# The context states of the four heads: taken ahead of the linear attention or inside its loop

## The chip, the cores and the metric

The kernel runs on one core of one Trainium2 chip. The core has a matrix engine (TensorE, PE in the rows), a vector engine (DVE), an activation engine (ACT), a general engine (GpSimd, POOL) and SyncE (SP), which here issues nearly all transfers. Each engine works through its own list of instructions in a fixed order and waits by semaphores for the others. The metric is the device time of one execution in microseconds (us).

## The reference, cut to what matters

Two transformer blocks run one after the other on 1024 tokens of width 1024, all in fp32. The change lies in the second block. Its mixer projects the 1024 tokens and, with the same weights, 256 context tokens. Four heads of linear attention (128 keys, 128 values each, forward and backward) start from a state that is worked out from the context tokens alone:

```python
def hg_forget(z, lb):
    k = (1.0 - lb) * jax.nn.sigmoid(-z)
    logf = jnp.log(jnp.maximum(lb + (1.0 - lb) * jax.nn.sigmoid(z), TINY))
    return k, logf

def gla_final_state(k, v, logf):                      # the context's state, one per head and direction
    suffix = jnp.minimum(lax.cumsum(logf, axis=1, reverse=True) - logf, 0.0)
    return jnp.einsum('bthk,bthv->bhkv', k * jnp.exp(suffix), v)

def gla_chunk_scan(q, k, v, logf, s0):                # linear attention that starts from that state
...
    def step(s, inp):
        qc, kc, vc, gc = inp
        b = jnp.cumsum(gc, axis=2)
        inter = jnp.einsum('bhtk,bhkv->bhtv', qc * jnp.exp(b), s)
        diff = b[:, :, :, None, :] - b[:, :, None, :, :]
        decay = jnp.where(causal, jnp.exp(jnp.minimum(diff, 0.0)), 0.0)
        scores = jnp.einsum('bhtk,bhtsk,bhsk->bhts', qc, decay, kc)
        intra = jnp.einsum('bhts,bhsv->bhtv', scores, vc)
...
    _, o = lax.scan(step, s0.astype(F32), (to_chunks(q), to_chunks(k), to_chunks(v), to_chunks(logf)))

def second_block(x, c, ctx, c_ctx, ada_w, ada_b, w_in, hg_lb, ...):
...
        px = modulate(x, mx[0], mx[1]) @ w_in[l]              # 1024 tokens
        pc = modulate(ctx, mc[0], mc[1]) @ w_in_ctx           # 256 context tokens
...
        s_f = gla_final_state(kf_c, v_c, lff_c)
        s_b = gla_final_state(flip(kb_c), flip(v_c), flip(lfb_c))
        mix_x = token_mixers(px, hg_x, s_f, s_b, *mix_args)   # linear attention | short conv | spatial gate
        x_new = layer_norm(ALPHA * x + mx[2] * (mix_x @ w_out[l]), ln1_g[l], ln1_b[l])
...
```

The state of a head needs the context's two gates (`z_f`, `z_b`), their logarithms summed from the far end, and the context's values `v_c`; nothing in it depends on the 1024 tokens.

## The kernel before

Every large product is made of three fp32r matmuls, from the high and the low part of each operand. A weight piece (`piece`, 128 x 1024, 512 KB) is loaded into one of two raw buffers `wr`, cast by ACT into its high part `wh`, and subtracted by POOL and DVE in turn into its low part `wl`; there are four buffers of `wh` and four of `wl`. `gemm_Z` takes one piece through all 1024 tokens: 48 matmuls of 128x512 into a two-bank tile `ps_Z`, of which there are two. `gemm_T` with `ctxT` takes a piece through the 256 context tokens: 24 matmuls of 128x256.

The second block's mixer is in three parts:

- `block2_in` norms and transposes the context (`ctxT`), makes the values of all heads for tokens and context (four pieces `w2_i`, ten output tiles `ps_z`; the tokens' values go to DRAM as `v_dr`, the context's stay as `vc`), then runs `spatial_gate` (four pieces `w2_sg`, eight tiles `ps_z`).
- `hgrn` is the loop over the four heads. Each head makes two gates from `w2_h[h, 0]` and `w2_h[h, 1]`, in `log_gate` (L1435 to L1441: copy out of PSUM on ACT, Tanh and Ln on ACT with steps of DVE between, a maximum on POOL). From them come `LB` and `LE` (log gates), `b` and `e` (sums of 128 tokens, by scans on DVE), `ks` (sum of two exponentials). Then it works out the context state: the gates `cps`, from the same two weight pieces while they are in SBUF, a second `log_gate` on 512 columns, two scans, an Exp, four transposes, and four matmuls into `st`, which ACT copies into the first slot of `S[0]` and the last of `S[1]`. The query and the output gate come from `w2_h[h, 2]` and `w2_h[h, 3]`; eight state updates follow. `gla_scores` makes, for each half `n` of the tokens, eight score products into `ps_lv`: one plain, and seven levels, each of four subtractions on DVE (`kk` from `LB`, `LE`; `qq` from `b`, `e`), two Exp on ACT, a multiplication by q on POOL (L1590), four fp32 matmuls (eight passes in the trace, L1593), and a masked copy on DVE. `gla_out` makes the output of a half (24 matmuls, a norm, four transposes). After head 2, and between scores and outputs of head 3, `short_conv` runs three products of `gemm_Z`.
- `block2_out` is the output GEMM with the weights `w_out2`, the residual rows `xs0` to `xs7` and a norm. The first five `xs` tiles are loaded at head 3, into the room where `ctxT` and `vc` were; the others follow in `block2_out`.

The tiles `LB`, `LE`, `b`, `e`, `ks`, `lf`, `q`, `og`, `vh`, `S` have one buffer each, `kk`, `qq`, `pt`, `kt` two. The order on each engine isn't that of the text: a scheduler lays the instructions out ahead of time by its own estimates, as far as data and buffers allow, so that products of the next head stand among the scores of this one. On the chip that order is fixed.

## Time and profile before

| what | us |
|---|---|
| median of 3 runs (2631.08 to 2636.38) | 2634.54 |
| the profiled execution | 2632.81 |
| its span in the trace | 2630.4 |
| values and spatial gate, 1232 to 1347 | 115 |
| first products and gates of head 0, 1347 to 1410 | 63 |
| the heads from the first score product, 1410 to 1815 | 405 |
| output GEMM's start, 1815 to 1862 | 47 |

The stretches are cut by hand in the trace, at the first score product of each head (1410, 1507, 1611, 1726) and where the outputs of head 3 go over to the output GEMM. The rows themselves stand in a section of their own below. In a windows view each engine's busy time in the stretch is read against the stretch's length: the engine near the length bounds it, and where none is near, the stretch goes by waits between engines.

### The profile page before, as it was taken

The numbers are of one execution on the slowest core, as the hardware profiler recorded it, in microseconds if no ns is written. First come the engines' busy times: TensorE is split into PE (matmuls) and PEld (weight loads), VectorE is DVE, ScalarE is ACT, GpSimd is POOL, SyncE is SP. The second block draws the span as 40 slices with busy tenths as digits, with TensorE's granted clock in tenths as the row PEclk, the third lists the DMA queues.
The fourth block names the chain that finished last, engine by engine and source line by source line (L and its number), as shares of the span: only waits on it lengthen the run. The fifth ranks groups of instructions, "written<-read, shape, count | busy, mean of one in ns | idle before, by whom it ended". The sixth has DMA issues, their size and how long they took to land.

```text
span 2630.4 us, 31222 instructions
## 1 busy us (share of the span) xinstructions
PE 2454.8 (93%) x11558; PEld 1996.0 (76%) x11558; DVE 1816.2 (69%) x2634; ACT 1002.2 (38%) x1473; POOL 1260.8 (48%) x769
## 2 busy tenths in 40 slices
PE   7989998989999989999998889998988999999998
PEld 3867776867788778788787677876766888887886
DVE  7387656588888896655157766678868777778645
ACT  3324462533333333224325545453234333333221
POOL 3253142368888862122125535445255777773222
PEclk8998798999999989999999989998999999999999
DMA  6522116213444348554120101113311222226442
GB/s 242 150 64 56 26 52 236 99 39 132 139 137 140 129 159 295 199 200 154 66 69 27 40 13 53 53 61 125 139 57 56 88 80 89 73 102 263 163 144 88
DMA packets 119015, 295.71 MB, mean 112 GB/s; under 512 B 24144, under 2 KB 38272, under 8 KB 118864
## 3 DMA queue, kind: packets, MB, share of 16 engines
q1 hardware_dynamic: 112528, 270.66, 30.5%
q10 hardware_dynamic: 6336, 23.07, 2.2%
q8 instruction: 91, 1.49, 0.2%
q14 instruction: 60, 0.49, 0.1%
HBM read 243.19 MB, written 49.31 MB: 111 GB/s over the span
## 4 chain that ended last, share of the span: by engine, by line
PE 65%; DVE 16%; DMA 6%; issue 5%; POOL 4%; ACT 4%; SPq 0%; POOLq 0%; ACTq 0%; DVEq 0%
PE ps_d L1199 15%; PE ps_U L1034 13%; PE ps_g L159 7%; PE ps_v L1034 7%; PE ps_Z L159 5%; PE ps_z L159 4%; PE ps_y L1034 3%; PE ps_lv L1593 2%; DVE cv L1262 1%; DMA wr<-in_w_down 1%; PE ps_s L607 1%; DVE wl L142 1%; DMA a<-in_w_mod 1%; PE ps_s L159 1%; DMA wr<-in_w_out 1%
## 5 line engine op out<-in xcount | busy, mean ns | idle before, releaser
L146 POOL TENSOR_TENSOR wl<-wr,wh 128x512 fp32r<-128x512 f32 (+1 forms) x158 | 291.7, 1858 | 446.6 <-ACT wh L145 446.6
L1034 PE MATMUL ps_U<-a,wh 128*128 128x512 f32 x1216 | 375.3, 390 | 3.9 <-DVE cv L1262 2.3
L1199 PE MATMUL ps_d<-wh,gh 128*128 128x512 f32 x704 | 276.3, 393 | 7.8 <-ACT gh L145 4.9
L1199 PE MATMUL ps_d<-wl,gh 128*128 128x512 f32 x704 | 275.7, 392 | 0.0
L1199 PE MATMUL ps_d<-wh,gl 128*128 128x512 f32 x704 | 270.5, 389 | 0.0
L1034 PEld LDWEIGHTS ps_U<-a,wh 128*128 128x128 f32 x1216 | 227.4, 188 | 53.2 <-issue 6.7
L159 PE MATMUL ps_g<-wh,a 128*128 128x512 f32 (+1 forms) x768 | 243.6, 395 | 17.1 <-ACT wh L140 11.7
L1034 PE MATMUL ps_U<-a,wl 128*128 128x512 f32 x608 | 235.8, 390 | 1.5 <-POOL wl L146 1.4
L1281 DVE SCALAR_TENSOR_TENSOR cv<-ps_U,cols,cv 128x945 f32<-128x945 f32 (+2 forms) x176 | 213.5, 1218 | 27.4 <-ACT cv L1273 24.7
L159 PE MATMUL ps_Z<-a,wh 128*128 128x512 f32 x704 | 227.4, 402 | 0.0
L146 POOL TENSOR_TENSOR wl<-S,wh 128x512 fp32r<-128x512 f32 (+1 forms) x114 | 213.3, 1886 | 20.1 <-ACT wh L145 19.4
L145 ACT CAST gh<-rx 128x1024 fp32r<-128x1024 f32 x88 | 89.9, 1047 | 275.1 <-issue 117.4
L159 PEld LDWEIGHTS ps_g<-wh,a 128*128 128x128 f32 x768 | 145.9, 199 | 48.1 <-ACT wh L140 12.6
L1199 PEld LDWEIGHTS ps_d<-wh,gh 128*128 128x128 f32 x704 | 133.0, 189 | 37.8 <-ACT gh L145 4.9
L145 ACT CAST wh<-S 128x512 fp32r<-128x512 f32 (+1 forms) x114 | 84.0, 761 | 202.8 <-POOL S L1114 142.1
L146 DVE TENSOR_TENSOR gl<-rx,gh 128x1024 fp32r<-128x1024 f32 x88 | 126.0, 1453 | 50.2 <-ACT gh L145 50.1
L159 PE MATMUL ps_g<-wl,a 128*128 128x512 f32 (+1 forms) x384 | 150.7, 392 | 5.2 <-POOL wl L142 5.2
L159 PEld LDWEIGHTS ps_Z<-a,wh 128*128 128x128 f32 x704 | 134.9, 194 | 26.5
L1199 PEld LDWEIGHTS ps_d<-wl,gh 128*128 128x128 f32 x704 | 133.0, 189 | 28.1 <-issue 0.9
L142 POOL TENSOR_TENSOR wl<-wr,wh 128x1024 fp32r<-128x1024 f32 x35 | 90.3, 2581 | 133.4 <-ACT wh L140 130.7
L1199 PEld LDWEIGHTS ps_d<-wh,gl 128*128 128x128 f32 x704 | 132.3, 188 | 27.4
L145 ACT CAST wh<-wr 128x512 fp32r<-128x512 f32 (+1 forms) x158 | 112.8, 736 | 91.9 <-PE ps_U L1034 40.2
(526 smaller groups left out, 5856.7 us busy)
## 6 DMA issues: line engine op xcount, KB each, us to landing
mw<-in_ada_w SPq DMA_DIRECT2D x112, 256.0 KB
wr<-in_w_up SPq DMA_DIRECT2D x44, 512.0 KB
rx<-g_w_up SPq DMA_DIRECT2D x44, 512.0 KB
wr<-in_f_up SPq DMA_DIRECT2D x44, 512.0 KB
rx<-g_f_up SPq DMA_DIRECT2D x44, 512.0 KB
g_w_up<-cv ACTq DMA_DIRECT2D x22, 512.0 KB
wr<-in_w_down SPq DMA_DIRECT2D x22, 512.0 KB
g_f_up<-cv ACTq DMA_DIRECT2D x22, 512.0 KB
```

Of the source, the lines that this page charges most:

```text
L142: (self.nc.gpsimd if self.turn else self.nc.vector).tensor_sub(lo, x, hi.bitcast(F32))
L145: self.nc.scalar.copy(hi, x)
L146: return eng.tensor_sub(lo, x, hi.bitcast(F32))
L159: self.nc.tensor.matmul(out, a, b, start=i == 0, stop=i == n - 1)
L607: nc.tensor.matmul(ps[:, gp, 1:P], wc[o:o + 64, r, gp, 1:9].rearrange("p k h -> p (k h)"), st[o:o + 64, r, gp, 0:P - 1], start=False, stop ...
L1034: self.nc.tensor.matmul(out, a, b, start=start and i == 0, stop=stop and i == 11, skip_group_check=True)
L1199: nc.tensor.matmul(ps, a[:, sl], b, start=q == 0 and j == 0, stop=q == NQ - 1 and j == 5, skip_group_check=True)
L1262: v.scalar_tensor_tensor(t[:, s:], us[part][:, :L - s], wt(j), t[:, s:], op0=ALU.mult, op1=ALU.add)
L1281: v.scalar_tensor_tensor(ov, s[:, r0 + di:r1 + di, c0 + dj:c1 + dj], wt(3 * (di + 1) + dj + 1), ov, op0=ALU.mult, op1=ALU.add)
L1593: nc.tensor.matmul(ps[:, j], ck(kk)[:, j], ck(qq)[:, j], start=True, stop=True)
```

## The change

`ctx_state` is a new function that does for one head what the loop did inside: it is called four times in `block2_in`, between the value product and `spatial_gate`, and puts the two states into DRAM (`s_dr[h]`, 128 KB). The loop loads them into `S` with two transfers per head. Since the weight pieces `w2_h[h, 0]` and `w2_h[h, 1]` are no longer shared, they are loaded, cast and subtracted once for the context and once for the tokens: eight pieces more. `ctxT` and `vc` are given up before the loop; `LB`, `LE` and `b` get a second buffer each. `e`, `lf`, `ks`, `q`, `og`, `vh` and `S` still have one. Only two `xs` tiles are loaded ahead, the other six in `block2_out`. The number of table loads on ACT goes from 46 to 51.

```diff
@@ block2_in @@
         wi = [self.piece(a["w2_i"][k]) for k in range(4)]
-        for i in range(NT + 2):
+        self.s_dr = [self.dr.tile([P, 2, P], F32, name=f"s{h}_dr") for h in range(4)]
+        for i in (NT, NT + 1, *range(NT)):
             ps = self.pt("z")
...
+        for h in range(4):
+            self.ctx_state(pool, h)
         self.spatial_gate(t3)
         self.psum(1, Z=2)
         es.close()
-        self.hgrn(self.pool(m3, "m3b"), ctx)
+        ctx.close()
+        self.hgrn(self.pool(m3, "m3b"))
@@ new function ctx_state @@
+    def ctx_state(self, pool, h):
+        nc, v = self.nc, self.nc.vector
+        half = lambda t: pool.tile([P, 512], F32, tag=t, name=t, bufs=2)
+        cps = self.pt("z")
+        for r in range(2):
+            self.gemm_T(cps[:, 256 * r:256 * r + 256], self.piece(self.a["w2_h"][h, r]), self.ctxT)
+        cf, ckk, cs = half("cf"), half("ck"), half("cs")
+        self.log_gate(cps, cf, ckk)
+        v.memset(cs[:, 255:257], 0.0)
+        on = self.ones[:, 0:1].to_broadcast([P, 255])
+        v.tensor_tensor_scan(cs[:, 254::-1], on, cf[:, 255:0:-1], 0.0, ALU.mult, ALU.add)
+        v.tensor_tensor_scan(cs[:, 257:512], on, cf[:, 256:511], 0.0, ALU.mult, ALU.add)
+        v.scalar_tensor_tensor(ckk, cs, 0.0, ckk, op0=ALU.min, op1=ALU.add)
+        nc.scalar.activation(ckk, ckk, AF.Exp)
+        tp = self.pt("tp", P, 4, P)
+        for j in range(4):
+            nc.tensor.transpose(tp[:, j], ckk[:, j * P:(j + 1) * P], self.ident)
+        kt = half("ckt").rearrange("p (c k) -> p c k", c=4)
+        nc.scalar.copy(kt, tp)
+        st = self.pt("o", P, 2, P)
+        hs = slice(h * P, (h + 1) * P)
+        for r in range(2):
+            for j in range(2):
+                nc.tensor.matmul(st[:, r], kt[:, 2 * r + j], self.vc[:, j, hs], start=j == 0, stop=j == 1)
+        s0 = pool.tile([P, 2, P], F32, tag="s0", name="s0", bufs=2)
+        nc.scalar.copy(s0, st)
+        nc.sync.dma_start(self.s_dr[h], s0)
@@ hgrn, the loop over heads @@
-            wf, zf = self.gemm_Z(a["w2_h"][h, 0])
-            cps = self.pt("lv")
-            self.gemm_T(cps[:, 0:256], wf, self.ctxT)
-            lf, LB = full("lf"), full("LB")
+            _, zf = self.gemm_Z(a["w2_h"][h, 0])
+            lf, LB = full("lf"), full("LB", 2)
...
-            b = full("b")
+            b = full("b", 2)
...
-            wb, zb = self.gemm_Z(a["w2_h"][h, 1])
-            self.gemm_T(cps[:, 256:512], wb, self.ctxT)
-            lf, LE = full("lf"), full("LE")
+            _, zb = self.gemm_Z(a["w2_h"][h, 1])
+            lf, LE = full("lf"), full("LE", 2)
...
-            cf, ckk, cs = half("cf"), half("ck"), half("ke")
-            self.log_gate(cps, cf, ckk)
...
-            nc.scalar.copy(S[0][:, 0], st[:, 0])
-            nc.scalar.copy(S[1][:, 7], st[:, 1])
+            S = [pool.tile([P, 8, P], F32, tag=f"S{r}", name="S", bufs=1) for r in range(2)]
+            for r in range(2):
+                nc.sync.dma_start(S[r][:, 7 * r], self.s_dr[h][:, r])
...
             if h == 3:
-                ctx.close()
...
-                self.xs = [xs_pool.tile([P, D], F32, name=f"xs{i}") for i in range(5)]
-                for i in range(5):
+                self.xs = [xs_pool.tile([P, D], F32, name=f"xs{i}") for i in range(2)]
+                for i in range(2):
                     nc.sync.dma_start(self.xs[i], self.x_dr[i])
@@ block2_out @@
-        self.xs += [xs_pool.tile([P, D], F32, name=f"xs{i}") for i in range(5, NT)]
+        self.xs += [xs_pool.tile([P, D], F32, name=f"xs{i}") for i in range(2, NT)]
...
-        self.out_gemm(pool, "w_out2", 2, lambda i: None if i < 5 else self.x_dr[i], self.pipe(norm, norm2, turn), (6, 7, 4, 0, 1, 2, 5, 3), ALPHA,
+        self.out_gemm(pool, "w_out2", 2, lambda i: None if i < 2 else self.x_dr[i], self.pipe(norm, norm2, turn), (6, 7, 4, 0, 1, 2, 5, 3), ALPHA,
```

What it moves is seen in three places. First ACT, where the scores of head 0 (`kk` and `qq` at L1588 and L1589 before, L1599 and L1600 after) meet the gates of head 1 (`LB`, `LE` and `lf` of `log_gate`). Before:

```order
L1588 ACTIVATE kk_11179<-kk_11179 128x512
L1589 ACTIVATE qq_11180<-qq_11180 128x512
L1588 ACTIVATE kk_11194<-kk_11194 128x512
L1589 ACTIVATE qq_11195<-qq_11195 128x512
L1435 COPY LB_11341<-ps_Z_11266 128x1024
L1588 ACTIVATE kk_11209<-kk_11209 128x512
L1435 COPY LE_11434<-ps_Z_11360 128x1024
L1589 ACTIVATE qq_11210<-qq_11210 128x512
L1608 ACTIVATE qq_11224<-b_10641 128x512
L1437 ACTIVATE lf_11340<-lf_11340 128x1024
L1611 ACTIVATE kk_11225<-kk_11225 128x512
L1438 ACT_TABLE_LOAD
```

After:

```order
L1599 ACTIVATE kk_11309<-kk_11309 128x512
L140 CAST wh_12189<-wr_12187 128x1024
L1600 ACTIVATE qq_11310<-qq_11310 128x512
L1439 COPY LB_11609<-ps_Z_11559 128x1024
L1599 ACTIVATE kk_11324<-kk_11324 128x512
L1600 ACTIVATE qq_11325<-qq_11325 128x512
L1554 COPY kt_11247<-ps_tp_11242 128x512
L1441 ACTIVATE lf_11608<-lf_11608 128x1024
L1442 ACT_TABLE_LOAD
L1442 ACTIVATE lf_11608<-lf_11608,half_80 128x1024
L1599 ACT_TABLE_LOAD
L1599 ACTIVATE kk_11339<-kk_11339 128x512
```

Before, the copies of head 1's gates stand among the last two levels of head 0, and their Tanh and Ln behind them; after, the copy of `LB` and the Tanh and Ln of `lf` stand among the levels of its first half, and the copy of `LE` right behind these.

Second PE, in the second score half of head 0 (`ps_lv` are score products, `ps_Z` products of the next head, `ps_tp` a transpose of an output). Before:

```order
L1618 MATMUL ps_o_11083<-S_10769,kk_11077 128x128
L1593 MATMUL ps_lv_11128<-qq_11120,kk_11119 128x128 x4
L1593 MATMUL ps_lv_11143<-qq_11135,kk_11134 128x128 x4
L1593 MATMUL ps_lv_11158<-qq_11150,kk_11149 128x128 x4
L1627 MATMUL ps_tp_11104<-ident_74,cf_11097 128x128 x4
L1593 MATMUL ps_lv_11173<-qq_11165,kk_11164 128x128 x4
L1593 MATMUL ps_lv_11188<-qq_11180,kk_11179 128x128 x4
L1593 MATMUL ps_lv_11203<-qq_11195,kk_11194 128x128 x4
L159 MATMUL ps_Z_11488<-a16_9333,wh_11484 128x512
```

After, where that half begins:

```order
L159 MATMUL ps_Z_11763<-a16_9333,wl_11760 128x512
L1604 MATMUL ps_lv_11421<-qq_11413,kk_11412 128x128 x4
L159 MATMUL ps_Z_11763<-a16_9333,wh_11759 128x512
L159 MATMUL ps_Z_11763<-a16_9334,wh_11759 128x512
L159 MATMUL ps_Z_11763<-a16_9333,wl_11760 128x512
```

and where it ends:

```order
L159 MATMUL ps_Z_11763<-a16_9557,wh_11759 128x512
L159 MATMUL ps_Z_11763<-a16_9558,wh_11759 128x512
L159 MATMUL ps_Z_11763<-a16_9557,wl_11760 128x512
L1604 MATMUL ps_lv_11466<-qq_11458,kk_11457 128x128 x4
L1604 MATMUL ps_lv_11481<-qq_11473,kk_11472 128x128 x4
L1604 MATMUL ps_lv_11496<-qq_11488,kk_11487 128x128 x4
L1604 MATMUL ps_lv_11511<-qq_11503,kk_11502 128x128 x4
L1627 MATMUL ps_o_11524<-vh_11180,pt_11405 128x128
```

Before, no `ps_Z` matmul stands between these six products; after, 45 stand between the half's second and fifth product and none among its last four. Counted from the first score product of a head to that of the next, 191, 192, 324 and 139 `ps_Z` matmuls stood in the four heads before, and 236, 192, 316 and 96 stand there after. The second half has no `ps_Z` matmul beside its last four products in head 0 and beside its last six in head 1 after the change; in head 2 both kernels have them beside all.

Third ACT in `block2_in`, behind the value product (`wh` are casts of weight pieces, `us` copies of the spatial gate, `ck` and `cf` the context's gate, `hT` and `vc` the context's transposed rows and values). Before:

```order
L140 CAST wh_10105<-wr_10103 128x1024
L381 ACTIVATE hT_9785<-ps_tp_9784,mod_sh_ac_6265,mod_sc_ac_7455 128x256
L1347 COPY vc_9794<-ps_z_10035 128x512
L1347 COPY vc_9794<-ps_z_10061 128x512
L140 CAST wh_10111<-wr_10109 128x1024
L1374 COPY us_10115<-ps_z_10117 128x256
L1374 COPY us_10115<-ps_z_10161 128x256
L1374 COPY us_10115<-ps_z_10205 128x256
L1374 COPY us_10115<-ps_z_10249 128x256
```

After:

```order
L140 CAST wh_10185<-wr_10183 128x1024
L140 CAST wh_10215<-wr_10213 128x1024
L1439 COPY ck_10153<-ps_z_10091 128x512
L1441 ACTIVATE cf_10152<-cf_10152 128x512
L1442 ACT_TABLE_LOAD
L1442 ACTIVATE cf_10152<-cf_10152,half_80 128x512
L140 CAST wh_10276<-wr_10274 128x1024
L140 CAST wh_10306<-wr_10304 128x1024
L1439 COPY ck_10244<-ps_z_10182 128x512
L1461 ACT_TABLE_LOAD
L1461 ACTIVATE ck_10153<-ck_10153 128x512
L1441 ACTIVATE cf_10243<-cf_10243 128x512
```

Two heads' context gates are under way at a time, with the casts of the next pieces among their steps.

## Rows read from the trace of the kernel before

**Rows 1.** Section 1 of the page: busy us (share of span) and instructions per engine.
```profile
PE 2454.8 (93%) x11558; PEld 1996.0 (76%) x11558; DVE 1816.2 (69%) x2634; ACT 1002.2 (38%) x1473; POOL 1260.8 (48%) x769
```

**Rows 2.** Windows: stretch, length, busy per engine (instructions), PEclk, DMA share, GB/s.
```profile
1232.00:1347.00 115.00, 112.04 (x523) 91.43 (x522) 40.47 (x130) 38.13 (x65) 26.84 (x20) 0.99 0.22 76
1347.00:1410.00 63.00, 60.42 (x296) 50.60 (x295) 39.87 (x57) 33.28 (x35) 26.83 (x13) 0.97 0.27 87
1410.00:1507.00 97.00, 82.21 (x465) 71.62 (x465) 69.40 (x114) 48.70 (x71) 47.01 (x28) 0.93 0.10 33
1507.00:1611.00 104.00, 88.60 (x487) 77.27 (x488) 71.76 (x116) 54.37 (x76) 50.90 (x29) 0.89 0.09 31
1611.00:1726.00 115.00, 109.23 (x616) 94.82 (x614) 79.26 (x123) 56.48 (x78) 53.83 (x29) 0.97 0.14 46
1726.00:1815.00 89.00, 75.81 (x411) 63.97 (x412) 68.28 (x105) 45.26 (x69) 45.38 (x30) 0.94 0.21 72
1815.00:1862.00 47.00, 37.14 (x147) 27.70 (x145) 32.82 (x40) 7.90 (x10) 9.52 (x5) 0.85 0.61 223
```

**Rows 3.** Windows, the four heads' loop as one stretch.
```profile
1410.00:1815.00 405.00, 355.85 (x1975) 307.68 (x1975) 288.70 (x457) 204.81 (x292) 197.12 (x113) 0.93 0.13 45
```

**Rows 4.** Windows inside the heads: score half, gates, head 2's dense middle.
```profile
1450.00:1470.00 20.00, 11.97 (x59) 10.55 (x58) 18.16 (x36) 10.41 (x17) 8.22 (x7) 0.74 0.03 13
1487.00:1515.00 28.00, 20.76 (x96) 16.44 (x94) 20.14 (x21) 19.05 (x22) 21.63 (x9) 0.99 0.16 52
1623.00:1715.00 92.00, 91.78 (x542) 80.71 (x541) 59.31 (x104) 44.26 (x63) 35.45 (x22) 1.00 0.13 44
```

**Rows 5.** Waits of PE in 1410:1815: us in total, times, longest.
```profile
PE ps_lv L1593 <- POOL qq L1590: 20.6, 12, 2.6
PE ps_lv L1593 <- ACT kk L1588: 14.1, 4, 5.0
```

**Rows 6.** Timeline of PE: start, us, instruction, [idle before <-releaser].
```profile
1452.80 1.16 PE L1593 MATMUL ps_lv<-qq,kk 128*128 128x128 f32 x8 [1.74 <-POOL qq L1590]
1466.19 2.07 PE L1593 MATMUL ps_lv<-qq,kk 128*128 128x128 f32 x8 [1.41 <-POOL qq L1590]
```

**Rows 7.** Chain of waits, in order of time: start, us, engine, tile, line, instructions.
```profile
1372.47 2.24 PE ps_lv L159 x19
```

**Rows 8.** Timeline of ACT, from head 0's last scores to the context chain's end.
```profile
1466.45 1.01 ACT L1435 COPY LB<-ps_Z 128x1024 f32<-128x1024 f32 x1 [1.66 <-DVE kk L1584]
1471.43 1.28 ACT L1438 ACT_TABLE_LOAD   x1
1503.26 0.57 ACT L1435 COPY ck<-ps_lv 128x512 f32<-128x512 f32 x1
1523.86 0.59 ACT L1499 COPY kt<-ps_tp 128x512 f32<-128x512 f32 x1 [0.47 <-PE ps_tp L1497]
1529.54 0.27 ACT L1506 COPY S<-ps_o 128x128 f32<-128x128 f32 x1 [4.57 <-PE ps_o L1504]
```

**Rows 9.** Timeline of DVE, head 1's forward sum.
```profile
1479.30 4.49 DVE L1471 TENSOR_TENSOR_SCAN b<-keep,lf 128x1024 f32<-128x1024 uint8 x1 [2.23 <-POOL lf L1441]
```

**Rows 10.** Timeline of POOL beside it: one weight subtraction.
```profile
1479.23 2.40 POOL L142 TENSOR_TENSOR wl<-wr,wh 128x1024 fp32r<-128x1024 f32 x1
```

**Rows 11.** Groups of DVE in 1507:1610: busy us, mean ns, idle before.
```profile
L1471 DVE TENSOR_TENSOR_SCAN b<-keep,lf 128x1024 f32<-128x1024 uint8 x1 | 2.3, 2292 | 2.2 <-POOL lf L1441 2.2
L1439 DVE SCALAR_TENSOR_TENSOR cf<-ck,cf 128x512 f32<-128x512 f32 x1 | 2.3, 2333 | 2.8 <-ACT cf L1438 2.8
L1440 DVE TENSOR_TENSOR ck<-cf,ck 128x512 f32<-128x512 f32 x1 | 1.6, 1648 | 0.0
L1436 DVE SCALAR_TENSOR_TENSOR cf<-ck 128x512 f32<-128x512 f32 x1 | 0.7, 692 | 0.5 <-ACT ck L1435 0.5
```

**Rows 12.** Waits in 1815:1862, where the mixed heads meet the output weights.
```profile
DVE wr L134 <- DMA wr<-in_w_out: 7.1, 4, 5.1
```

More of the change, by code (lines that the diff above doesn't have):

```diff
@@ L1441, in log_gate, with hgrn @@
         nc.gpsimd.tensor_scalar(t, t, LN_TINY, None, op0=ALU.max)
-    def hgrn(self, pool, ctx):
+    def ctx_state(self, pool, h):
[25 more added lines that the diff above has]
+        nc.sync.dma_start(self.s_dr[h], s0)
+    def hgrn(self, pool):
         nc, v, g, a = self.nc, self.nc.vector, self.nc.gpsimd, self.a
@@ L1485, in hgrn @@
             g.tensor_add(LE, LE, e)
-            cf, ckk, cs = half("cf"), half("ck"), half("ke")
-            self.log_gate(cps, cf, ckk)
-            v.memset(cs[:, 255:257], 0.0)
-            on = self.ones[:, 0:1].to_broadcast([P, 255])
-            v.tensor_tensor_scan(cs[:, 254::-1], on, cf[:, 255:0:-1], 0.0, ALU.mult, ALU.add)
-            v.tensor_tensor_scan(cs[:, 257:512], on, cf[:, 256:511], 0.0, ALU.mult, ALU.add)
-            v.scalar_tensor_tensor(ckk, cs, 0.0, ckk, op0=ALU.min, op1=ALU.add)
-            nc.scalar.activation(ckk, ckk, AF.Exp)
-            tp = self.pt("tp", P, 4, P)
-            for j in range(4):
-                nc.tensor.transpose(tp[:, j], ckk[:, j * P:(j + 1) * P], self.ident)
-            kt = half("kt", 2).rearrange("p (c k) -> p c k", c=4)
-            nc.scalar.copy(kt, tp)
-            st = self.pt("o", P, 2, P)
-            hs = slice(h * P, (h + 1) * P)
-            for r in range(2):
-                for j in range(2):
-                    nc.tensor.matmul(st[:, r], kt[:, 2 * r + j], self.vc[:, j, hs], start=j == 0, stop=j == 1)
-            S = [pool.tile([P, 8, P], F32, tag=f"S{r}", name="S", bufs=1) for r in range(2)]
-            nc.scalar.copy(S[0][:, 0], st[:, 0])
-            nc.scalar.copy(S[1][:, 7], st[:, 1])
+            S = [pool.tile([P, 8, P], F32, tag=f"S{r}", name="S", bufs=1) for r in range(2)]
+            for r in range(2):
+                nc.sync.dma_start(S[r][:, 7 * r], self.s_dr[h][:, r])
+            hs = slice(h * P, (h + 1) * P)
             if h == 3:
-                ctx.close()
                 self.x5 = ExitStack()
                 xs_pool = self.pool(self.x5, "xs5", "right")
-                self.xs = [xs_pool.tile([P, D], F32, name=f"xs{i}") for i in range(5)]
-                for i in range(5):
+                self.xs = [xs_pool.tile([P, D], F32, name=f"xs{i}") for i in range(2)]
+                for i in range(2):
                     nc.sync.dma_start(self.xs[i], self.x_dr[i])
```

## The prediction

> **What bounds the kernel now.** I read the engines' shares first, then the windows by stage, then the heads from inside (windows, waits, timelines). PE is busy 93% of the whole span [rows 1], so a saving must either take work off PE or fill one of its few holes. The windows say where the holes are. The values and the spatial gate are PE's: 112.04 of 115 us, while ACT and DVE work a third of it; so are the 63 us ahead of the first scores, with 60.42 [rows 2]. The four heads are not: in 405 us PE works 355.85, DVE 288.70, and the granted clock is 0.93 [rows 3]. That leaves 49 us of holes, and more PE time than at full clock.
>
> The reader is to see that the same loop goes in two ways. In the middle of head 2, 92 us long, PE works 91.78 at clock 1.00; in the second score half of head 0, PE works 11.97 of 20 us at 0.74 while DVE works 18.16; around the gates of head 1 it has 20.76 of 28 [rows 4]. The waits name the first kind of hole: 20.6 us for `qq` from POOL and 14.1 for `kk` from ACT, 34.7 of the 49 [rows 5]. These are score levels with no other product beside them. One level then takes (1466.19 - 1452.80) / 4 = 3.35 us, of which the first's eight passes are 1.16 (the last's 2.07 are stretched by the falling clock) [rows 6]; about 2.2 us are lost per bare level. A level with `ps_Z` matmuls beside it loses nothing.
>
> Why are levels bare? Head 1's log gate can only begin when head 0 has read `LB` for the last time: the copy into `LB` waits 1.66 us for the last `kk` and comes at 1466.45 [rows 8], so head 1's products that wait for a free `ps_Z` come late too. Second buffers undo that, and the order shows it.
>
> **The heads.** PE loses the context work of heads 1 to 3 in this stretch (head 0's gemm lies ahead of it). One head's is 48 matmuls of 128x256 at 2.24/19 = 0.118 us [rows 7], 5.7, and four transposes and eight passes more, which I put at 1.1 by the 1.16 of a score product's eight passes: 6.8. Three times 6.8 is 20, and PE's work falls from 355.85 to 335.
>
> For the holes I count levels in the order: 4 bare ones remain in head 0, 6 in head 1, none in head 2. Ten times 2.2 is 22 us of holes where there were 49, so 335 + 22 = 357, which is 48 less. The clock gives a little, from 0.93 toward the 1.00 of head 2's dense middle [rows 3, 4]; most of its fall lies in the bare levels that stay, so I take 2 us. That is -50. The worse end: besides the 22 us, the 14 us of other holes (49 - 34.7) stay and the clock doesn't move: 371, or -34. The better end: all holes go, 336, or -69. I take -50 since it is nearest to what is counted; head 2's dense middle shows that a head can go without holes when products lie beside every level.
>
> **Ahead of the scores.** Head 0's context gemm, 5.7 us, leaves 63 us in which PE works 60.42 [rows 2]. The gates of head 0 are a chain over ACT, DVE and POOL that the loss does not shorten, though ACT has four steps less to do between them. Between 0 and -6; I take -3.
>
> **The values and the spatial gate.** All four heads' context work comes here, 4 x 6.8 = 27 us, into a stretch that PE fills to 97%, so it counts in full. The log gate, scans and Exp have room on ACT (38.13 of 115) and DVE (40.47) [rows 2]: per head six DVE instructions, 0.7 to 2.3 us each [rows 11]. What isn't free is their place. ACT runs its list in order, and in the new order the casts of the next weight pieces stand between `ck`, Tanh, a table load of 1.28 us [rows 8], Ln and Exp. A cast behind a gate step waits for DVE, and PE for the cast. Each of the eight new pieces also needs a raw buffer, a transfer on SP's queue (behind the stores of `v_dr`), a cast, and on every other piece 2.40 us of POOL [rows 10]; a piece feeds PE for 24 x 0.118 = 2.8 us only, where a `w2_sg` piece feeds it for eight tiles. So a piece must arrive every 2.8 us, and that is about what POOL takes for one of two. I charge 0 to 20 us of holes and take 9, one missed piece or gate step per head. Together +36.
>
> **The output GEMM.** Six `xs` tiles are loaded here instead of three, 1.57 MB more, 7 us at the 223 GB/s that this start moves now [rows 2]. The weights' waits of 7.1 us [rows 12] are there already. In SP's order the last output weights have no more in front of them than before; the added rows come behind. Between 0 and +7, I take +1. The loads of `S` cost SP two small transfers per head beside `vh`, which waits for the same last outputs, so I put them at 0; if they are late, the wait falls on the state updates, not on scores. The second buffers cost no instruction.
>
> **The sum.** -50 - 3 + 36 + 1 = -16, against the profiled 2632.8: 2617. The median of the runs is 1.7 us above the profiled one, so about **2618** for the median.
>
> **A rule that speaks against it.** Head 1's forward sum took 4.49 us, from 1479.30 on [rows 9], beside a POOL subtraction of 2.40 us that began at 1479.23 [rows 10]; in the next head the same scan took 2.29 [rows 11]. It lost 2.2 us, nearly all of POOL's time. The Trainium skill, SBUF — State Buffer, section Who interferes with whom, says that a DVE instruction with two SBUF inputs contends with a GpSimd instruction that reads SBUF, and that whoever issues first shuts the other out. By that rule, the trace agrees, DVE and POOL together have less room than their separate shares show.
>
> **The rivals.** *DVE and POOL bind.* If work packed closer only makes more such collisions, DVE's share stays where it is: 288.70 / 405 = 0.713 [rows 3]. DVE loses four context gates, each 2.3 + 1.6 + four of 0.7 = 6.7 us [rows 11], 27 in all, and the loop takes 262 / 0.713 = 367 us, -38; nothing comes ahead of the scores, and block 2's start still costs +36 and the output +1: 2632, or 2633 for the median, no change. For it: the 18.16 of 20 us of DVE in the bare half, the stretched scan. Against it: head 2's middle, where PE is full and DVE has 59.31 of 92 [rows 4].
>
> *The context stage starves PE, and the kernel is slower.* One context chain took from 1503.26 (copy of `ck`) to 1529.54 (copy into `S`), 26 us, with score steps in between [rows 8]; its own steps are some 15: ACT's copies, Tanh, table loads, Ln and Exp about 6, DVE 6.7, POOL's maximum and PE the rest. If PE finds nothing beside two of the four chains, because the spatial gate's pieces are cast behind them, the stage grows by 27 + 30 = 57 us: -50 - 3 + 57 + 1 = +5, 2640 for the median; if beside all four, 27 + 60, +35, 2670. Half way between, nearer the first: 2650. It decides when the stretch grows by more than 52 us. For it: ACT's single order with table loads between two heads' gates. Against it: two buffers of each gate tile, and 115 us in which ACT has 77 free.
>
> *All holes close.* -69 for the heads is the end; with the 27 us without holes and -3 ahead: -45 to -38, some 2592. For it: head 2's middle. Against it: the ten bare levels that stand in the order.
>
> *It doesn't do what it says.* `lf`, `e` and `ks` still have one buffer, and could hold the gates back as `LB` did. Against it: in the new order the copy and the Tanh and Ln of `lf` stand among head 0's first half already. The heads would lose the 20 us of context work and no hole: -20 - 3 + 36 + 1 = +14, about 2648; a small part of the slower case.
>
> **How the numbers follow.** The forecast has 0.50 (2607 to 2629), DVE and POOL 0.20 (2633), the starved stage 0.17 (2640 to 2670), all holes closed 0.13 (2592). About 0.2%, 5.3 us, is what a measurement of this kernel can tell from no change. Faster: 0.13 and nearly all of the 0.50, 0.62. Same: 0.20 and little of the others, 0.20. Slower: 0.18. For the range, 2592 to 2643: it reaches down to the closed holes and up past the first end of the starved stage, and leaves out half of the one and most of the other.
>
> **What would show it.** In the profile of the changed kernel: the four heads take about 355 us with PE's waits for `qq` and `kk` near 22 instead of 34.7, at a clock above 0.95; head 1's copy into `LB` comes before head 0's first score half is over. The stage with values and spatial gate takes about 151 us, PE works 139 of it. The output GEMM's start stays at 47. The forecast is wrong if the heads stay above 371, with DVE's share still at 0.71 (then the shared access), or if the stage exceeds 167 with PE waiting for weight pieces or `ps_tp` (then the starved chain).

## The result: slower by 27 us

The changed kernel takes 2660.2 us (median of 6 runs, 2646.5 to 2666.2) where the kernel before takes 2632.8 beside it (median of 6): ratio 1.011 (95% interval 1.0078 to 1.0142). The forecast was 2618, the range 2592 to 2643. The profiled execution took 2657.47 us, its span is 2655.2, its granted clock 0.950.

Section 1 of the page of the changed kernel answers [rows 1] (busy us, share of the span, instructions); the share of PE is the same:

```profile
PE 2463.0 (93%) x11558; PEld 2003.6 (75%) x11558; DVE 1842.6 (69%) x2638; ACT 1016.2 (38%) x1482; POOL 1271.8 (48%) x773
```

Profiles of kernels that are the same up to there reach the end of the first block anywhere from 1217 to 1238 us. So I compare from that point on (the last L1199 matmul) in three stretches, windows on each: **lead** (to the first score product), **loop** (to the last output product of head 3) and **rest**. Columns are as in [rows 2]. The kernel before:

```profile
1231.60:1409.50 177.90, 172.37 (x814) 141.84 (x813) 80.20 (x185) 71.49 (x101) 53.76 (x31) 0.98 0.24 80
1409.50:1818.10 408.60, 359.45 (x2008) 311.21 (x2006) 291.73 (x460) 207.13 (x296) 198.32 (x114) 0.93 0.14 46
1818.10:2630.40 812.30, 769.74 (x3339) 626.54 (x3337) 573.84 (x606) 256.43 (x322) 406.38 (x260) 0.98 0.32 114
```

The changed kernel:

```profile
1223.80:1447.30 223.50, 202.08 (x1012) 168.33 (x1011) 102.42 (x212) 96.06 (x133) 67.59 (x39) 0.96 0.27 90
1447.30:1846.20 398.90, 345.86 (x1835) 296.70 (x1833) 289.46 (x440) 196.57 (x272) 200.31 (x112) 0.91 0.13 44
1846.20:2655.20 809.00, 767.32 (x3314) 624.49 (x3313) 569.04 (x603) 256.26 (x320) 405.34 (x258) 0.97 0.32 115
```

The lead is 45.6 us longer, the loop 9.7 shorter, the rest 3.3 shorter: +32.6, of which 7.8 are hidden in this pair by an earlier start. The forecast had +33, -50 and +1. In the loop PE works 13.6 us less, but stands idle 53 us where it stood 49, and the granted clock is lower (0.91 after 0.93). The cut between loop and rest is one in time, not in work: of the 384 matmuls of the output GEMM (`ps_g`), 61 stand in the loop before and 85 after the change, so loop and rest are best read together: -13. By heads, answering the four of [rows 2]:

```profile
1447.00:1557.00 110.00, 90.10 (x471) 76.90 (x470) 81.98 (x116) 57.74 (x77) 57.80 (x31) 0.89 0.11 35
1557.00:1653.00 96.00, 80.96 (x427) 70.38 (x426) 64.48 (x109) 49.18 (x67) 50.43 (x28) 0.86 0.11 35
1653.00:1757.00 104.00, 100.17 (x543) 86.45 (x542) 76.22 (x117) 54.11 (x71) 52.37 (x28) 0.97 0.16 52
1757.00:1842.00 85.00, 70.73 (x381) 59.07 (x380) 66.34 (x100) 34.92 (x58) 38.74 (x25) 0.94 0.17 56
```

Head 0 takes 110 us instead of 97, with 236 `ps_Z` matmuls in it instead of 191; heads 1 to 3 win 8, 11 and 4. PE's waits in the lead, where [rows 2] showed next to none, and in the loop, answering [rows 5]:

```profile
PE ps_Z L159 <- ACT LB L1439: 5.3, 1, 5.3
PE ps_z L159 <- POOL wl L142: 4.2, 4, 2.5
PE ps_z L159 <- ACT wh L140: 3.5, 2, 2.1
...
PE ps_lv L1604 <- POOL qq L1601: 26.5, 14, 5.9
PE ps_lv L1604 <- ACT kk L1599: 2.6, 1, 2.6
```

The waits for scores fell from 34.7 to 29.1 us, not to 22, and others grew beside them (6.1 us for `pt`, 3.7 for `e`, 3.4 for `cf`, all from DVE).

### The profile page after: what moved, and what is told of

It is laid out like the page before. It is cut to its first block, busy times and chain, and to the rows that moved or that the text cites. A ratio compares the mean times of both kernels' runs of the same rounds, so it can differ in the third digit from the quotient of the medians.

```text
span 2655.2 us, 31293 instructions
## 1 busy us (share of the span) xinstructions
PE 2463.0 (93%) x11558; PEld 2003.6 (75%) x11558; DVE 1842.6 (69%) x2638; ACT 1016.2 (38%) x1482; POOL 1271.8 (48%) x773
## 5 line engine op out<-in xcount | busy, mean ns | idle before, releaser
L1199 PE MATMUL ps_d<-wh,gh 128*128 128x512 f32 x704 | 276.4, 393 | 6.4 <-ACT gh L145 4.9
L1199 PE MATMUL ps_d<-wl,gh 128*128 128x512 f32 x704 | 275.8, 392 | 0.0
L1199 PE MATMUL ps_d<-wh,gl 128*128 128x512 f32 x704 | 270.5, 389 | 0.0
L142 POOL TENSOR_TENSOR wl<-wr,wh 128x1024 fp32r<-128x1024 f32 x39 | 100.8, 2585 | 138.0 <-ACT wh L140 137.6
L1199 PEld LDWEIGHTS ps_d<-wh,gh 128*128 128x128 f32 x704 | 132.9, 189 | 36.6 <-ACT gh L145 6.3
L1199 PEld LDWEIGHTS ps_d<-wl,gh 128*128 128x128 f32 x704 | 133.0, 189 | 27.9 <-issue 0.9
L1199 PEld LDWEIGHTS ps_d<-wh,gl 128*128 128x128 f32 x704 | 132.3, 188 | 27.7
```

What stands on the lines that cost most here:

```text
L142: (self.nc.gpsimd if self.turn else self.nc.vector).tensor_sub(lo, x, hi.bitcast(F32))
L1199: nc.tensor.matmul(ps, a[:, sl], b, start=q == 0 and j == 0, stop=q == NQ - 1 and j == 5, skip_group_check=True)
```

## The experiments

All runs in one table: median, its ratio to the kernel before measured beside it (95% interval; that kernel's medians lie between 2631.2 and 2634.7), the three stretches of the profiled run, cut as above, and how many of the output GEMM's 384 matmuls stand in the loop.

| run | us | ratio | lead | loop | rest | `ps_g` in loop |
|---|---|---|---|---|---|---|
| before | 2632.8 | 1 | 177.9 | 408.6 | 812.3 | 61 |
| changed | 2660.2 | 1.0078 to 1.0142 | 223.5 | 398.9 | 809.0 | 85 |
| e1_single | 2657.0 | 1.0050 to 1.0121 | 223.0 | 392.0 | 808.6 | 85 |
| e2_nostate | 2617.4 | 0.9901 to 0.9952 | 183.6 | 391.4 | 809.5 | 85 |
| b_nostate | 2617.8 | 0.9917 to 0.9981 | 181.6 | 391.9 | 809.3 | 85 |
| e4_ctxdve | 2655.1 | 1.0059 to 1.0118 | 217.2 | 396.0 | 808.1 | 85 |
| e3_qqdve | 2659.9 | 1.0057 to 1.0159 | 222.7 | 395.2 | 807.4 | 85 |
| e5_notable | 2643.4 | 1.0013 to 1.0071 | 221.4 | 384.1 | 805.7 | 85 |
| g1_oneterm | 2635.5 | 1.0001 to 1.0046 | 216.0 | 374.0 | 809.2 | 85 |
| g2_nomult | 2632.8 | 0.9967 to 1.0020 | 223.1 | 353.4 | 824.2 | 37 |
| b_warm | 2633.1 | 0.9976 to 1.0026 | 177.7 | 408.5 | 814.2 | 61 |
| b_late | 2633.8 | 0.9980 to 1.0031 | 176.6 | 412.7 | 812.5 | 61 |
| h1_kx | 2649.0 | 1.0023 to 1.0086 | 218.6 | 379.6 | 813.4 | 61 |
| h4_single_kx | 2646.8 | 1.0042 to 1.0085 | 218.8 | 388.3 | 814.5 | 49 |
| h2_kx_e | 2653.0 | 1.0051 to 1.0106 | 221.7 | 377.5 | 820.1 | 49 |
| h3_kx_le | 2653.5 | 1.0047 to 1.0096 | 219.7 | 375.5 | 825.5 | 37 |
| g3_noscale | 2628.7 | 0.9960 to 1.0003 | 177.6 | 408.2 | 812.0 | 61 |
| g4_noscale_le | 2616.9 | 0.9918 to 0.9976 | 177.6 | 396.1 | 818.0 | 37 |

**Taking the change apart.** First only the moved context states, with single buffers and five `xs` tiles:

```diff
-            lf, LB = full("lf"), full("LB", 2)
+            lf, LB = full("lf"), full("LB")
```

(and the same for `LE` and `b`.)

> The changed kernel with one buffer again for LB, LE and b, and five xs tiles loaded ahead again: of the change only the context states ahead of the loop are left. In the profile of the changed kernel the four heads take 395 us (405 before) and the way to the first scores 215 (178 before). The prediction's theory (second buffers fill holes, 30 of the 50 us that the heads were to lose): the heads go up by 30, about 2690 us. Rival 1, the gates only moved (with second buffers a gate of the next head stands inside this head's score levels and stops them for 8.5 us each, so what the end of a head wins its beginning loses): the buffers are worth nothing, 2650 to 2665. Rival 2, DVE and POOL shut each other out more since the buffers packed them closer (kk subtractions rose from 549 to 712 ns): the mean of these falls back to about 550 ns and the heads to about 385, 2645 to 2652.

2657.0, not told from the changed kernel's 2660.2: the second buffers are worth nothing here. Then the changed kernel without context states, and the kernel before without them:

```diff
-        for h in range(4):
-            self.ctx_state(pool, h)
...
-                nc.sync.dma_start(S[r][:, 7 * r], self.s_dr[h][:, r])
+                nc.gpsimd.memset(S[r][:, 7 * r], 0.0)
```

> The changed kernel without the context states: ctx_state isn't called (no second loads of the eight pieces, no gemm, gate, scans, transposes or state products), the first slots of S are set to zero by POOL instead of loaded. It prices the stage that was moved. The traces of the two kernels put 37.5 us on it, 21 of PE work and 16 of holes: 2622 us. If the context work was mostly hidden and the loss is the heads' own, 2640 or more. The heads stay at 395 by both rivals on them, since nothing in the loop changes but two transfers; if the loads of S delay the loop, the heads fall below 390.

> The kernel before without the context states (no context gemm, gate, scans, transposes or state products in the loop; the first slots of S set to zero by POOL). It prices the context work where it stood. The prediction's count (27 us of PE work, 6 of them ahead of the first scores, all on the path): 2607 us. Filler theory (in the loop the context work stands largely in time that PE has to spare, so that it costs there far less than its PE time, while ahead of the loop it costs all of it and its holes): 2617 to 2625. Against the changed kernel without context states (2617) it also prices the second buffers alone: rival 1 (gates only moved) says the same time within 5 us; the prediction's theory says 30 us more here, 2647.

Lead and loop of these three, in windows (e1_single, e2_nostate, b_nostate):

```profile
1222.00:1445.00 223.00, 201.84 (x1012) 168.12 (x1011) 102.27 (x212) 96.17 (x133) 67.45 (x39) 0.96 0.29 97
1445.00:1837.00 392.00, 342.06 (x1834) 293.05 (x1833) 273.99 (x440) 193.53 (x270) 189.88 (x112) 0.93 0.14 45
```

```profile
1223.00:1406.60 183.60, 169.60 (x771) 138.06 (x770) 73.90 (x180) 65.65 (x94) 51.54 (x33) 0.97 0.25 83
1406.60:1798.00 391.40, 346.14 (x1835) 297.71 (x1833) 282.47 (x440) 196.82 (x272) 201.16 (x118) 0.90 0.14 44
```

```profile
1232.90:1414.50 181.60, 169.32 (x771) 138.25 (x770) 73.76 (x180) 65.28 (x93) 51.23 (x33) 0.97 0.28 93
1414.50:1806.40 391.90, 340.77 (x1834) 291.88 (x1833) 276.80 (x440) 193.50 (x270) 191.18 (x118) 0.93 0.14 44
```

Without context states both kernels take the same time, 2617 and 2618, and their loops 391.4 and 391.9: second buffers alone, 0 (with the states, 398.9 with them and 392.0 without). The context work is priced in both places. In the loop it costs 408.6 - 391.9 = 16.7 us, and in the lead nothing (177.9 with head 0's part, 181.6 without): 13, with the rest, which is 3 shorter, 16, and 14 in the medians. Ahead of the loop it costs 223.0 - 181.6 = 41 or 223.5 - 183.6 = 40. The price is some 13 in one place and 40 in the other: that is the 27 us.

**The stage.** The low parts of the context's pieces on DVE alone (`turn` decides who subtracts):

```diff
+            was, self.turn = self.turn, True
             self.gemm_T(cps[:, 256 * r:256 * r + 256], self.piece(self.a["w2_h"][h, r]), self.ctxT)
+            self.turn = was
```

> The changed kernel with the low parts of the eight context pieces made by DVE alone (1.2 us each, where POOL takes 2.4 for every other one). In the changed kernel PE waits in the moved stage 4.2 us for POOL's low parts and 3.5 for the casts. If a piece's way through POOL sets the stage's holes: -4 to -8 us, 2652 to 2656, and the waits for POOL gone. If the transfers and ACT's order set them, the waits turn into waits for casts and the time stays at 2660.

2655.1, within what was expected if POOL sets the holes, but too small a step for the medians to separate. The lead is 6.3 us shorter; in the waits of its lead POOL is gone and the chain of the context gate is next:

```profile
1233.50:1450.70 217.20, 199.55 (x1011) 166.80 (x1011) 107.23 (x216) 96.17 (x134) 58.20 (x35) 0.98 0.28 93
```

```profile
PE ps_tp L1466 <- ACT ck L1463: 3.3, 2, 2.2
PE ps_z L159 <- DVE wl L142: 0.7, 1, 0.7
```

So of the stage's 40 us, 32 are PE work (202.08 - 169.60), and the holes are 7 to 9.

**What holds the loop.** Two thirds of the products of the heads left out:

```diff
+            if one:
+                for k in range(KT):
+                    self.nc.tensor.matmul(ps[:, n * 512:n * 512 + 512], w[0][:, k * P:(k + 1) * P], self.aT[n][0][:, k],
+                                          start=k == 0, stop=k == KT - 1)
+                continue
```

> The changed kernel with the heads' products (four per head) made of one matmul instead of three: the terms with the low parts are left out, 128 matmuls of 128x512 a head, 29 us of PE work each, 117 in all; casts, low parts and transfers stay. If PE's work bounds the heads (the prediction: its work plus what bare levels cost): 90 to 115 us less, 2545 to 2570. If the chain over DVE, ACT and POOL bounds them (rival 1) and PE's products lie beside it wherever they stand: 15 us ahead of the first scores, where PE does bind, and 15 to 40 in the loop, 2605 to 2630.

```profile
1449.60:1823.60 374.00, 276.62 (x1433) 239.65 (x1433) 281.79 (x434) 194.55 (x269) 195.69 (x111) 0.82 0.13 42
```

PE works 69 us less in the loop, the loop is 25 shorter, and 25 are saved in all. PE stands idle 97 of the 374 us that are left, at a granted clock of 0.82 after 0.91, so part of what is left takes longer. PE's work alone isn't what bounds the loop. The same was asked from the other side, PE's idle time filled with copies of the score products (second half of heads 0 and 1 of the kernel before):

```diff
+            if i >= 0 and warm:
+                pd = self.pt("lv", P, 4, P)
+                for _ in range(2):
+                    for j in range(4):
+                        nc.tensor.matmul(pd[:, j], ck(kk)[:, j], ck(qq)[:, j], start=True, stop=True)
```

> The kernel before with each level's score product of the second half of heads 0 and 1 issued three times, the second and third into a tile that nobody reads: 14 levels, mostly bare ones, 1.8 us more of PE work each at full clock, in time in which PE waits 2.2. It asks what the falling clock costs around bare levels: the 24 output matmuls behind such a half run at half clock, 0.43 instead of 0.22 us each. If that is a cost of its own: the clock stays at 1.00 in these halves and the loop loses 5 us a head, 2623 to 2628. If the clock doesn't matter since the levels are DVE's, ACT's and POOL's: 2632 to 2640; if the copies come in the way of the levels: up to 2660.

The loop of this kernel, two of its levels on PE (L1593 the product, L1598 the copies), and the first subtraction of a later level on DVE:

```profile
1398.10:1806.60 408.50, 372.44 (x2233) 325.79 (x2231) 288.42 (x460) 210.15 (x299) 198.38 (x114) 0.97 0.14 46
```

```profile
1448.31 1.16 PE L1593 MATMUL ps_lv<-qq,kk 128*128 128x128 f32 x8 [0.41 <-POOL qq L1590]
1449.30 1.95 PE L1598 MATMUL ps_lv<-qq,kk 128*128 128x128 f32 x16
1451.66 1.16 PE L1593 MATMUL ps_lv<-qq,kk 128*128 128x128 f32 x8 [0.41 <-POOL qq L1590]
```

```profile
1454.72 0.53 DVE L1584 TENSOR_TENSOR kk<-LB,b 128x256 f32<-128x256 f32 x1 [1.12 <-PE ps_lv L1598]
```

The clock of the loop rises from 0.93 to 0.97, PE works 13 us more, and the loop stays at 408.5: filling PE's idle time costs nothing, and a higher clock with it wins nothing. The levels stay 3.35 us apart (1448.31 to 1451.66), the very figure of [rows 6], but that the two agree is luck: `kk` has two buffers, and here DVE waits 1.12 us ahead of a level's first subtraction until the copies have read the one that it writes, while in the kernel before the product itself took up to 2.07 us at the fallen clock [rows 6]. A level's way goes round DVE, ACT, POOL and PE, and two levels are under way at a time; what the fallen clock alone costs it isn't shown.

Three runs took something out of that way in the changed kernel: the multiplication moved to DVE or left out, and the table loads of the loop's gates left out.

```diff
-                g.tensor_tensor(qq, qq, qn, op=ALU.mult)
+                v.tensor_tensor(qq, qq, qn, op=ALU.mult)
```

> The changed kernel with the multiplication of qq by q on DVE instead of POOL, 64 of 512 columns, of 1.4 to 1.5 us each on POOL. Rival 2 (DVE and POOL shut each other out): the kk subtractions fall from 0.70 us to near 0.42, which gives back about as much DVE time as the multiplications cost there (56 x 0.68 = 38 us), each level loses 0.8 us of its chain, and the heads take 395 - 20 to 395 - 50: 2610 to 2640 us. Rival 1 (the gates stop the levels on DVE, which works in order): DVE is the engine that everything waits for, its busy time rises by 38 and the heads with it: 2665 to 2695 us.

> The changed kernel without the multiplication of the levels' qq by q on POOL (64 of some 1.5 us). Nothing is put on another engine for it, other than where it went to DVE. If the chain over DVE, ACT and POOL bounds the heads: most of a level's 1.3 us in the levels that stand bare or nearly so, and less collision of DVE with POOL, 40 to 80 us less, 2580 to 2620. If PE bounds them: 0 to 15 less, 2645 to 2660.

```diff
-        nc.scalar.activation(t, t, AF.Ln, bias=self.half, scale=0.5)
+            nc.scalar.activation(t, t, AF.Copy, scale=-0.5)
```

> The changed kernel with the Ln of the loop's eight log gates replaced by a scaled copy on ACT of the same size, so that no table has to be changed for it (36 table loads in the program instead of 51); the gates' values are then others, the work of every other engine is the same. Rival 1 (the gates stop the levels): each gate is shorter by two loads of 1.28 us, 2.6, and eight of them by 20: the heads take about 375, 2640 us. Rival 2 (DVE and POOL): ACT isn't what is short, 2655 to 2660 us.

The loops of g2_nomult, e5_notable and e3_qqdve:

```profile
1461.00:1814.40 353.40, 321.06 (x1785) 277.79 (x1784) 252.62 (x434) 194.19 (x268) 114.33 (x54) 0.95 0.14 44
```

```profile
1438.90:1823.00 384.10, 338.60 (x1835) 291.74 (x1833) 291.89 (x440) 182.87 (x261) 200.11 (x112) 0.92 0.14 46
```

```profile
1451.90:1847.10 395.20, 341.74 (x1834) 293.83 (x1833) 299.67 (x496) 195.91 (x272) 122.51 (x56) 0.92 0.14 44
```

Left out, the multiplication shortens the loop by 45 us (27 in all: the rest is 15 longer, with 48 matmuls of the output GEMM in it that stood in the loop); the table loads by 15 (17 in all), one for one nearly, since 15 loads of 1.28 us are 19. Moved to DVE, it gives nothing: neither rival's figure came. The groups of DVE in the loop, changed kernel and e3_qqdve:

```profile
L1595 DVE TENSOR_TENSOR kk<-LB,b 128x256 f32<-128x256 f32 x54 | 38.5, 712 | 0.0
L1596 DVE TENSOR_TENSOR kk<-LE,e 128x256 f32<-128x256 f32 x56 | 38.3, 689 | 2.3 <-POOL LE L1515 2.3
```

```profile
L1601 DVE TENSOR_TENSOR qq<-qq,q 128x512 f32<-128x512 f32 x56 | 40.5, 727 | 11.7 <-ACT qq L1600 10.5 <-POOL q L1530 0.8
L1596 DVE TENSOR_TENSOR kk<-LE,e 128x256 f32<-128x256 f32 x56 | 33.1, 596 | 4.6 <-POOL LE L1515 4.6
L1595 DVE TENSOR_TENSOR kk<-LB,b 128x256 f32<-128x256 f32 x54 | 26.2, 485 | 0.0
```

DVE took 40.5 us of new work and its busy time rose by 10 (289.5 to 299.7): 30 us of stretching went. They were real, but more work than that had come to DVE, and the way of a level had only changed engines. g2_nomult takes POOL's work and the stretching away together (DVE's busy time falls from 289.5 to 252.6), so no run prices the stretching alone.

The context gate's place in the row of the gates doesn't matter either (in the kernel before, its steps written behind `q` and `og`): 2633.8.

> The kernel before with the context state's steps written behind the query and the output gate of the same head instead of ahead of them; the gemm stays where it was. It asks whether the context gate's place in the row of gates matters. If the context gate stands in the way of the query and of the first levels (it holds ACT with two table loads): the way from gate to first score gets shorter by up to 5 us a head, 2615 to 2630. If it is filler already: no change, 2630 to 2640.

**What the second buffers run into.** Three rows of the changed kernel, on DVE, ACT and POOL, between heads 0 and 1:

```profile
1547.12 0.75 DVE L1640 SCALAR_TENSOR_TENSOR ck<-ps_tp,cols,og 128x512 f32<-128x512 f32 x1 [3.92 <-PE ps_tp L1638]
...
1547.90 1.06 ACT L1513 ACTIVATE og<-LE 128x1024 f32<-128x1024 f32 x1 [5.60 <-DVE ck L1640]
...
1549.04 2.35 POOL L1514 TENSOR_TENSOR ks<-ks,og 128x1024 f32<-128x1024 f32 x1 [6.57 <-ACT og L1513]
```

Head 1's exponential `kx` is written into `og`, which has one buffer, and waits until head 0's last output has read it; `ks`, and head 1's first score at 1557.2, come behind. So `kx` got a tile of its own, with second buffers (one `xs` tile ahead) and without (four):

```diff
-            kx = full("og")
+            kx = full("kx")
```

> The changed kernel with a tile of its own for the exponential of LE (kx), which shares og's one buffer otherwise; its room comes from one xs tile less loaded ahead. If og's buffer is what holds the next head back: the row of products between heads (68 ps_Z matmuls in the order, 19 to 28 here) and the wait of 5.6 us per head go, 5 to 12 us a head in heads 1 to 3, 2625 to 2645. If the chain over DVE, ACT and POOL is simply full: 2655 to 2662.

> The changed kernel with single buffers of LB, LE and b (four xs tiles ahead) and a tile of its own for kx. If kx and the second buffers are worth something only together (the next head is held by whichever buffer is still single): as with single buffers alone, 2650 to 2660, and the run with both below it by 15 or more. If kx alone is the holder: as the run with both.

> As the run with a tile of its own for kx, and a second buffer for e; no xs tile is loaded ahead. If e's one buffer is the next holder (the scan into e waits for head 0's last reader of e): 2 to 5 us a head more than without it, 2612 to 2635. If the chain is full by then: as without it, plus 0 to 7 for the xs tiles.

> The changed kernel with a tile of its own for kx, without the scaling of q on POOL and with the sum into LE on DVE (what gave 14 us on the kernel before). If POOL's part of the chain holds the heads in both kernels: some 10 to 15 us below the run with kx alone, 2612 to 2632.

The loops of h1_kx and h4_single_kx:

```profile
1436.00:1815.60 379.60, 335.98 (x1821) 287.88 (x1821) 281.03 (x439) 193.44 (x271) 203.27 (x111) 0.92 0.14 43
```

```profile
1453.50:1841.80 388.30, 336.26 (x1809) 286.70 (x1809) 283.89 (x437) 191.23 (x266) 193.26 (x110) 0.93 0.13 41
```

In the loops the tile gives 19 us with second buffers and 4 without, as if the two belonged together; loop and rest taken together, it is 15 shorter and 2 longer. The medians don't say so: 2649.0 and 2646.8, both some 10 below what they were without it, and for h4_single_kx the intervals overlap (1.0042 to 1.0085, without the tile 1.0050 to 1.0121). The traces lean here: that of h1_kx is of the fastest of its ten executions (2631.3), that of h4_single_kx of the slowest (2658.1). A second buffer for `e`, or less work for POOL, takes 2 to 4 us more off the loop, and the rest, where 12 and 24 more matmuls of the output GEMM then stand, grows by 7 and 12; the medians (2653.0, 2653.5) are no lower. So `og` is one of the tiles that hold the next head, worth some 10 us with second buffers; that the second buffers pay once it is gone is seen in one trace each and stays open.

**A version faster than both.** On the kernel before, POOL's scaling of q folded into the norm's column, and the sum into `LE` on DVE:

```diff
-            g.tensor_scalar(q, q, P ** -0.5, None, op0=ALU.mult)
...
-            g.tensor_add(LE, LE, e)
+            v.tensor_add(LE, LE, e)
```

> The kernel before without POOL's scaling of q in the loop (2.8 to 4.7 us a head): the factor goes into the column of the output norm once, and its square into the norm's mean. If the chain from gates to first score runs over POOL, as its sums of ks and LE stand behind that scaling: 3 to 4.6 us a head, 2613 to 2622. If PE bounds the gates' part: no change, 2628 to 2636.

> As the run without the scaling of q, and the sum into LE (2.4 to 2.7 us on POOL, a head) moved to DVE, 1.2 us. By the chain: 1 to 2 us a head more than without it, 2606 to 2618. If DVE is what is short there: as without it or some 5 slower.

2628.7 and 2616.9. The first alone is not told from no change; with both, the kernel is 14 us faster than before (0.9918 to 0.9976) and 43 below the changed one. Its loop:

```profile
1404.50:1800.60 396.10, 352.04 (x1985) 305.05 (x1983) 281.32 (x460) 204.06 (x291) 175.88 (x105) 0.94 0.13 43
```

Two POOL instructions stood between the gates and the first scores of each head, the scaling and the sum into `LE`. With one gone and the other on DVE the loop is 12.5 us shorter; 24 matmuls of the output GEMM went from it into the rest, which is 5.7 longer, so loop and rest together win 7 in this trace, where the medians have 14.

## Why the prediction was wrong

**What bounds the heads: the step that failed.** "A level with `ps_Z` matmuls beside it loses nothing" is true of PE and false of the time. I read the 3.35 us of a bare level as 1.16 of work and 2.2 of hole, and meant to win the hole by putting products there: 22 us of holes where there were 49. There are 53. The level goes its own way over DVE, ACT, POOL and PE, and the products that fill its hole are taken from elsewhere: 192 per head are all there are, and between the last product of head 0 or 1 and the first of the next head, where they had covered the gates, 68 stand instead of 91. g1_oneterm shows that PE's work beside that way counts for a third, 25 of 69 us. The dense middle of head 2 [rows 4] misled me: PE was full there because `short_conv` adds three products, not because the levels went faster (head 2 takes 115 us, heads 0 and 1 take 97 and 104).

Two readings went into the 22 as well. The 14.1 us for `kk` are not bare levels: they are four waits, each ahead of the first level of a head, behind its gates, as this one of head 1 in the kernel before:

```profile
1515.12 2.04 PE L1593 MATMUL ps_lv<-qq,kk 128*128 128x128 f32 x8 [5.05 <-ACT kk L1588]
```

And head 3, with 14.3 us of idle PE in the changed kernel, wasn't counted.

**The gates came earlier and gave it back.** The order did what it said: head 1's copy into `LB` ran at 1467.13, in head 0's first half. These rows of DVE and ACT show what it costs there:

```profile
1471.75 1.21 DVE L1440 SCALAR_TENSOR_TENSOR lf<-LB 128x1024 f32<-128x1024 f32 x1
...
1476.55 1.22 DVE L1443 SCALAR_TENSOR_TENSOR lf<-LB,lf 128x1024 f32<-128x1024 f32 x1 [2.57 <-ACT lf L1442]
...
1479.59 0.73 DVE L1608 COPY_PREDICATED pt<-lev,ps_lv 128x512 f32<-128x512 uint8 x1
1480.22 0.41 DVE L1595 TENSOR_TENSOR kk<-LB,b 128x256 f32<-128x256 f32 x1
```

```profile
1474.08 1.28 ACT L1442 ACT_TABLE_LOAD   x1
...
1481.04 1.28 ACT L1599 ACT_TABLE_LOAD   x1 [4.52 <-DVE kk L1596]
```

From 1471.75 to 1480.22 no `kk` is made: DVE holds its order while ACT changes the table for Ln, and ACT changes it back before the next Exp. Head 0's first half took 45.2 us (1447.3 to 1492.5) where it took 31.6; its second half and the gates behind it 64.7 instead of 65.8, as `og` held head 1 back (51.6 in h1_kx, where `kx` has its own tile). I had seen the single buffers as a rival that makes nothing move; they let the gates move and held the end.

**The terms.** Heads: -50 forecast, -9.7 measured; the 20 us for the context work came as 17 (e1_single, b_nostate), the 30 for second buffers as 0, in one pair of traces 7 lost. Lead: -3 for head 0's context work, and it was free there: without it the lead is 3.7 longer (b_nostate). It had stood where PE waits for the copy of head 0's first gate out of `ps_Z`; without it, that wait is bare:

```profile
PE ps_Z L159 <- ACT LB L1435: 5.7, 1, 5.7
```

The 5.3 us for `LB` in the changed kernel's lead are the same wait, and no hole of the moved stage. Without context states the lead of the changed kernel is 5.7 longer than before (e2_nostate); with the stage's 40 that makes the 45.6. Stage: +36, with 27 of PE work and 9 of holes; measured 40, with 32 and 7 to 9. I had 6.8 us a head, and 32 / 4 is 8. Rest: +1, measured -3.3, with 24 matmuls of the output GEMM fewer in it. So the sum failed by the heads, and by some 12 us ahead of them; what I didn't see is that work taken out of a stretch that isn't PE's gives back less than it costs in one that is: 13 against 40.

**The rivals.** The starved stage, which was to be the slower end, priced a time near the result but isn't the cause: it decides above 52 us of growth, and the lead grew by 45.6, with 7 to 9 us of holes in the stage instead of 30. *DVE and POOL bind* foretold DVE's share (289.46 / 398.90 = 0.726, forecast 0.713) and the stretched instructions, but not the time: 2633 for the median, with heads of 367 us. By the sign that I had set, heads above 371 with DVE's share still at 0.71, it would be the cause. The runs don't settle it. Against it: h4_single_kx has 10 us more of DVE's busy time than e1_single in a loop 4 us shorter. For it: DVE's share of the loop lies between 0.70 and 0.76 in every run here, whatever was taken out. e3_qqdve can't decide, since it takes away 30 us of stretching and puts 40.5 us of work on the same engine. Its 4.49 us scan [rows 9] has its like in the changed kernel, on POOL and DVE:

```profile
1466.77 2.41 POOL L142 TENSOR_TENSOR wl<-wr,wh 128x1024 fp32r<-128x1024 f32 x1 [6.23 <-ACT wh L140]
```

```profile
1467.05 2.41 DVE L1595 TENSOR_TENSOR kk<-LB,b 128x256 f32<-128x256 f32 x1
```

A subtraction of 0.41 us takes until POOL is done. The Trainium skill, SBUF — State Buffer, section Who interferes with whom, says that the second of the two blocks until the first is done; the trace agrees. What DVE's lost time costs the loop stays open.

*All holes close* would have needed the levels themselves to be shorter. *It doesn't do what it says*, the heads losing the 20 us of context work and no hole, comes nearest to what the heads did (e1_single: 17 lost); with the lead 45.6 us longer instead of 33, that makes the kernel slower.

## What to carry to other kernels

Before work is moved off a busy stretch, price it in both places by leaving it out in both: PE work in a stretch held by a chain over other engines cost a third to a half of itself here (25 of 69 us, 13 of the 27 that were forecast), and in a stretch that PE fills all of itself and some holes (40, with 32 of work). A hole on an engine isn't time to be won unless that engine's work is what ends last; double one engine's work or take two thirds away, and see whether the stretch moves. A second buffer lets the next round begin, but the round is held by whichever buffer is still single, and steps that begin earlier stand in the way of what they join on engines that work in order.

## What the runs showed that I had not expected

- 69 us less of PE work in the loop shortened it by 25, at a granted clock of 0.82.
- 13 us more of PE work in the loop, and a granted clock of 0.97 instead of 0.93 with it, left its length where it was (b_warm, 408.5 and 408.6).
- The end of the first block, up to which these kernels are alike, lay between 1217 and 1238 us in the profiled runs, as wide as most of the differences here; stretches measured from that point agree within 3 us between kernels that share them (lead 177.9, 177.7, 177.6 and 177.6 in four kernels that have it unchanged).
